# Paired up-projection forms made of unscaled activations during the output projection, with the row factor applied to each pair's results

## The chip, the cores and the metric

The kernel runs on one core of one Trainium2 chip. A core has a matrix engine (PE), whose weight loads (PEld) overlap its matmuls, a vector engine (DVE), a scalar engine (ACT), a general engine (POOL), and a queue engine (SP) that issues transfers. The engines run side by side, each through its own list of instructions in order, and wait for each other by semaphores. Matmul results land in PSUM, in banks of 128 x 512 float32; everything else is in SBUF, with the weights read from HBM. The metric is the device time of one execution in microseconds (us), lower being better.

## The reference

Two layers of a bidirectional encoder over 512 tokens of 1024 features, in float32. What matters here is the second half of a layer and the projection ahead of it:

```python
    x = x + merged @ w_out[l]                      # output projection
    hf = rms_norm(x, ffn_norm_g[l])                # per token: x * rsqrt(mean(x^2) + eps) * g
    u = depthwise_conv(hf @ ffn_w_up[l], ffn_conv_w[l], ffn_conv_b[l])
    u_gate, u_val = u[..., :D_FF], u[..., D_FF:]   # D_FF = 2816
    x = x + (jax.nn.silu(u_gate) * u_val) @ ffn_w_down[l]
```

The convolution runs along the tokens, width 3, one filter per column. Ahead of this stand an input projection, latent attention, grouped-query attention and a pooling branch, merged by gates. The row factor of the norm, rsqrt(mean(x^2) + eps), is one number per token; it can be taken out of the up-projection and put on its result.

## The kernel before

Activations lie feature-major: 8 blocks of 128 features by 512 tokens, `XM`. Each float32 operand of a matmul is held as two halves, a rounded high part and the rest as a low part (`wh`/`wl` or `fh`/`fl` for weights, `HH`/`HL` for the normed input, `ah`/`al` for activations), and each product is three matmuls (`mm3`): high by high, high by low, low by high.

**Output projection.** Eight output blocks of 24 matmuls each. After each block, `norm_steps` runs a chain: residual into `XM` (DVE), high half of XM x g (ACT) and the square (ACT), low half (DVE), sum of squares (POOL). The result is `HH`/`HL`, scaled by the gain g and not yet by the row factor. When all eight squares are summed, `norm_begin` and `norm_finish` make the row factor, `rbc`.

**Up-projection.** Two times 2816 columns are 22 channels (`c`) of 128 gate and 128 value columns each. The channels stand in groups, `SIZES`, and are computed in one of two ways:

- *Plain*, the first group of 6: for gate and value each 8 blocks of 3 matmuls on 512 tokens (`feat_major`), 24 matmuls. `scale` multiplies the result by `rbc` on its way out of PSUM.
- *Paired*, the other 16: a 2 x 2 scheme of fast matrix multiplication over two feature blocks, two halves of the tokens, and gate against value. Seven products (`FORMS`: "11", "12", "1", "22", "2", "4", "3") of 4 x 3 matmuls on 256 tokens take the place of eight. The weights' sums for the forms are made on DVE (`w_form`); the activations' forms (`tf`) are made once a layer by `build_forms`, while the plain channels run: the 8 blocks are normed whole (`hn`), four sums a pair of blocks (`tt`) and the splits follow, with 12 of the 28 forms kept in the `m` tiles, which the attention used before, and 16 in slots.

After either, `convolve` does the convolution (ACT, then two on DVE), the gate (ACT), the product (DVE) and the split of the activation: high half on ACT, low half on POOL.

**Down-projection.** A group's down products are dealt out between the products of the next group's pairs (`_ffn`), and those of the last group come at the end. `keep_act` places a channel's activation: groups 1 to 3 in `HH`/`HL`, group 0 in slots, and the last group's in other tiles.

**Weights.** They come from HBM on SP's queue in an order written out by `_stream`: a raw tile holds two units of 128 x 512, the four raw parts of a pair are tiles of 512 of their own (at most 8 held at once). Each unit is split before use: a "p" unit by a copy on ACT and a subtract on DVE or POOL (`pick`), a "u" unit by two copies on ACT and an accumulating transfer that POOL issues (`by_transfer`). In the plain channels all units are "u". `wnext` splits `LA` = 3 units ahead of use, and `LAF` = 6 where forms are near; six pairs of split tiles rotate.

**Order.** The order on each engine's list is set when the program is written: a model clock (`Clock`) with costs per instruction says when a chain's next step is due, and that is when the instruction is emitted. `PLACE` and `KEEP` place activations and hold back the last downs of a group.

Of the kernel before, what the change touches and what calls it, by code (L numbers as in the profile page):

```python
# [42 lines left out]
LA, LAF = 3, 6  # L43
SIZES = (6, 5, 4, 4, 3)
PLACE = {1: 0, 2: 5, 3: 0}
# [100 lines left out]
def _stream():  # L146


    pieces, slots, units, alone = [], [], [], []
    for kind, *u in _layer_units() * L:  # L150
# [9 lines left out]
        if len(slots) <= KC or alone[-1] or slots[-1] + u[0] > 1024:  # L160
            slots.append(0)
            alone.append(False)
        pieces.append((len(slots) - 1, slots[-1], u[0]))
# [158 lines left out]
def trunk(ctx: ExitStack, tc: tile.TileContext, x, w, prm, gb, cst, out):  # L322
# [101 lines left out]
    def w_split():  # L424
# [22 lines left out]
        if pi + 1 == len(pieces) or pieces[pi + 1][0] > sl:  # L447
# [105 lines left out]
    def norm_steps(gen, kc, g, sq):  # L553
# [17 lines left out]

        return [hi, lo, add]
# [94 lines left out]
    def layer(l, sq, xsrc):  # L667
# [900 lines left out]
        tags = ("acc", "ST", "AV", "mi", "S")  # L1568
        for m in range(KC):
# [13 lines left out]
            chain(resid, *norm_steps(G2, m, col(PRM_FG + m), sq))  # L1583
# [9 lines left out]
        forms = {}  # L1593

        def build_forms():
            for q in range(4):
                m = mp.tile([P, 3, T], F32R, tag="m", name=f"tf{l}{q}")
                forms["raw", q] = m
                for n, name in enumerate(("11", "12", "4")):
                    forms[name, q] = m[:, n, :]  # L1600
                for name in ("1", "22", "2", "3"):
                    forms[name, q] = slot("tf", F32R)[:, :T]
            hn, tt = {}, {}
            lo, hi = slice(0, 256), slice(256, 512)

            def normed(k):
                hn[k] = slot("hn")[:, :T]
                V.scalar_tensor_tensor(hn[k], XM[:, k, :], col(PRM_FG + k), fin["rbc"][:, :T], ALU.mult, ALU.mult)
                done("hn", l, k)

            def sums(q):
# [395 lines left out]
```

## Time and profile before

| What | Value |
|---|---|
| Median of 3 runs | 1577.67 us (1575.77 to 1579.9) |
| The profiled execution's own time | 1578.39 us |
| Its span, first to last instruction | 1576.6 us |
| PE busy | 1548.2 us, 98% |
| DVE / ACT / POOL busy | 1111.4 / 1034.4 / 859.7 us |
| Mean granted PE clock | 0.997 |
| Output projection, layer 0 and 1 | 388 to 432 us, 1170 to 1213 us |
| Plain channels, layer 0 and 1 | 432 to 503 us, 1213 to 1287 us |
| Pairs with dealt downs, layer 0 and 1 | 503 to 765 us, 1287 to 1551 us |

A row of a group of instructions names the line of the kernel, the engine, the operation, what is written and read, shapes and count; then busy us and the mean ns of one; then the engine's idle time just before such instructions and what ended it. A row of the timeline gives start and length in us, and in brackets the idle time before it. Nearly every instruction has the line of a helper (L283 an activation, L290 a two-tensor operation, L294 a three-operand one, L302 a product by scalars, L421 the accumulating transfer, L390 a weight load, L508 a matmul), so the tile's name tells which work it is.

### The profile page before, as it was taken

How to read it: one execution, taken by the hardware profiler on the slowest of the kernel's cores; microseconds unless marked ns; L12 is line 12 of the kernel's file. 1: busy time of each engine (PE TensorE's matmuls, PEld its weight loads, DVE VectorE, ACT ScalarE, POOL GpSimd, SP SyncE). 2: the span in 40 equal slices, each digit the busy share in tenths (PEclk: the TensorE clock that was granted, in tenths of full speed). 3: DMA queues.
4: the chain of work that ended last, by engine and by line, in shares of the span. 5: the costliest groups of instructions: out<-in, count | busy, mean ns of one | idle time of the engine just before them, and what ended most of it. 6: DMA issues, size and time to landing. Idle time of an engine off the chain costs nothing.

```text
span 1576.6 us, 23997 instructions
## 1 busy us (share of the span) xinstructions
PE 1548.2 (98%) x8193; PEld 1338.6 (85%) x8193; DVE 1111.4 (70%) x1816; ACT 1034.4 (66%) x1932; POOL 859.7 (55%) x868
## 2 busy tenths in 40 slices
PE   9999989999999999999999999899999999999999
PEld 8888878888877999998888888788888779999987
DVE  6867886875278777777656688778652877777774
ACT  5557776763478777777655587666535787777773
POOL 3974876854653433333588658668546443333333
PEclk9999999999999999999999999999999999999999
DMA  5432224324489887886535322343244798888853
GB/s 205 126 114 74 74 85 144 107 67 134 113 179 230 200 193 185 205 183 132 135 117 141 100 74 74 96 138 101 70 146 123 170 229 192 192 198 187 194 113 101
DMA packets 127563, 222.36 MB, mean 141 GB/s; under 512 B 29648, under 2 KB 51664, under 8 KB 127440
## 3 DMA queue, kind: packets, MB, share of 16 engines
q1 hardware_dynamic: 90864, 162.93, 33.2%
q0 software_dynamic: 31680, 57.69, 21.3%
q8 instruction: 64, 1.05, 0.3%
q10 hardware_dynamic: 4896, 0.21, 0.2%
q14 instruction: 59, 0.48, 0.1%
HBM read 149.41 MB, written 13.63 MB: 103 GB/s over the span
## 4 chain that ended last, share of the span: by engine, by line
PE 74%; DVE 13%; ACT 6%; issue 4%; POOL 2%; DMA 1%; SPq 0%; ACTq 0%; DVEq 0%; POOLq 0%
PE ps_acc L508 32%; PE ps_AV L508 14%; PE ps_ST L508 12%; PE ps_S L508 8%; PE ps_mi L508 8%; DVE a L294 2%; DVE XM L290 2%; ACT wh L283 1%; DVE wl L290 1%; DVE u L290 1%; DVE mgl L290 1%; ACT mgh L283 1%; DVE hn L294 1%; ACT fh L283 1%; DVE tf L290 1%
## 5 line engine op out<-in xcount | busy, mean ns | idle before, releaser
L290 POOL TENSOR_TENSOR wl<-raw,wh 128x512 fp32r<-128x512 f32 (+3 forms) x241 | 305.0, 1275 | 224.6 <-ACT wh L283 206.5
L283 ACT ACTIVATE wh<-raw 128x512 fp32r<-128x512 f32 (+2 forms) x457 | 269.2, 605 | 56.9 <-DVE raw L290 12.9
L421 POOL DMA_DIRECT2D wl<-raw x124 | 110.9, 919 | 290.3 <-ACT wl L283 106.0
L508 PE MATMUL ps_acc<-HH,wl 128*128 128x512 f32 x416 | 164.3, 395 | 6.2 <-DMA wl<-raw 6.2
L508 PE MATMUL ps_acc<-HH,wh 128*128 128x512 f32 x416 | 164.1, 394 | 3.4 <-DVE vm L290 2.9
L294 DVE SCALAR_TENSOR_TENSOR a<-u,prm,a 128x511 f32<-128x511 f32 x176 | 142.8, 811 | 32.2 <-ACT a L283 31.2
L508 PE MATMUL ps_acc<-HL,wh 128*128 128x512 f32 x416 | 163.5, 393 | 0.0
L421 POOL DMA_DIRECT2D fl<-raw x96 | 85.2, 887 | 105.7 <-ACT sx L283 47.0
L290 DVE TENSOR_TENSOR wl<-raw,wh 128x512 fp32r<-128x512 f32 (+2 forms) x93 | 92.4, 995 | 60.6 <-ACT wh L283 60.5
L283 ACT ACTIVATE a<-u,prm 128x512 f32<-128x512 f32 x88 | 71.5, 815 | 86.6 <-DVE u L290 86.2
L298 DVE TENSOR_REDUCE nm<-ps_S 128x1 fp32r<-128x512 f32 x128 | 87.6, 685 | 36.0 <-PE ps_S L508 34.8
L508 PEld LDWEIGHTS ps_acc<-HH,wl 128*128 128x128 f32 x416 | 78.8, 189 | 24.9 <-DMA wl<-raw 7.9
L508 PEld LDWEIGHTS ps_acc<-HH,wh 128*128 128x128 f32 x416 | 79.0, 190 | 19.8 <-issue 4.4
L508 PE MATMUL ps_AV<-tf,wh 128*128 128x256 f32 x512 | 94.8, 283 | 0.0
L508 PE MATMUL ps_acc<-tf,wh 128*128 128x256 f32 x512 | 94.4, 282 | 0.0
L508 PE MATMUL ps_ST<-tf,fh 128*128 128x256 f32 x512 | 94.2, 281 | 0.0
L508 PEld LDWEIGHTS ps_acc<-HL,wh 128*128 128x128 f32 x416 | 78.9, 190 | 16.3
L508 PEld LDWEIGHTS ps_acc<-tf,wh 128*128 128x128 f32 x512 | 83.9, 191 | 5.3
L508 PEld LDWEIGHTS ps_AV<-tf,wh 128*128 128x128 f32 x512 | 81.4, 190 | 2.6
L283 ACT ACTIVATE wl<-wh 128x512 fp32r<-128x512 f32 x124 | 78.5, 633 | 3.9
L508 PEld LDWEIGHTS ps_ST<-tf,fh 128*128 128x128 f32 x512 | 79.4, 190 | 0.0
L508 PE MATMUL ps_acc<-tf,wl 128*128 128x256 f32 x256 | 72.4, 283 | 0.0
(417 smaller groups left out, 4844.8 us busy)
## 6 DMA issues: line engine op xcount, KB each, us to landing
raw<-w SPq DMA_DIRECT2D x162, 512.0 KB, 3.7
raw<-w SPq DMA_DIRECT2D x136, 256.0 KB, 4.2
wl<-raw POOLq DMA_DIRECT2D x124, 256.0 KB, 4.3
fl<-raw POOLq DMA_DIRECT2D x96, 256.0 KB, 5.4
raw<-w SPq DMA_DIRECT2D x14, 384.0 KB, 3.0
XM<-x SPq DMA_DIRECT2D x16, 256.0 KB, 3.2
dtq<-tr SPq DMA_DIRECT2D x16, 192.0 KB, 1.9
dtk<-tr SPq DMA_DIRECT2D x16, 192.0 KB, 2.0
```

The lines of the kernel that those rows point to most:

```text
L283: return self.eng.activation(out, in_, func, **k)
L290: return self.eng.tensor_tensor(out, *a)
L294: return self.eng.scalar_tensor_tensor(out, *a)
L298: return self.eng.tensor_reduce(out, in_, *a, **k)
L421: nc.gpsimd.dma_start(f(lo), r, accum_op=ALU.add)
L508: PE.matmul(o, lhsT=lhsT, rhs=rhs, start=start, stop=stop, skip_group_check=again)
```

## The change

- One channel a layer goes from plain to paired: groups of 5, 5, 5, 4, 3 instead of 6, 5, 4, 4, 3, so 5 plain channels and 17 pairs.
- The forms are made during the output projection, after each second block, from XM x g without the row factor. `norm_steps` first makes the whole product (`whole`, a product by a column on DVE), then its halves. Forms "11", "12" and "4" are the halves in `HH`/`HL` themselves; the sums and the other 16 forms follow as before.
- Each pair's gate and value results, u and v, are multiplied by `rbc` (`scale`, DVE) before the convolution.
- Activations (down inputs) go into the `m` tiles, six channels' places, and otherwise into wide tiles and slots; `HH`/`HL` stay as they are until the last pair.
- The activations' low halves are made on DVE instead of POOL.
- In the plain channels the second unit of each half channel is a "p" unit; units are split `LAP` = 4 ahead while a "u" is near; and the eight raw tiles of the first two pairs are loaded one after each plain half channel from the second on.

```diff
-SIZES = (6, 5, 4, 4, 3)
-PLACE = {1: 0, 2: 5, 3: 0}
+LA, LAP, LAF = 3, 4, 6
+SIZES = (5, 5, 5, 4, 3)
+PLACE = (0, 5, 0, 5, 0)
+ROOM = 6
...
         if tok[0] == "u":
-            r += [("u", T)] * 2
+            r += [("u", T), ("p", T), ("next",)]
...
+        if kind == "next":
+            plain = (plain + 1) % (2 * SIZES[0])
+            if plain and plain >= 2 * SIZES[0] - 8:
+                early.append(len(slots))
+                slots.append(T)
+                alone.append(True)
+            continue
         if kind == "f":
             if u[1] == FORMS[0]:
-                first = len(pieces)
+                first, fresh = len(pieces), True
                 for _ in range(4):
+                    if early:
+                        pieces.append((early.pop(0), 0, T))
+                        continue
                     pieces.append((len(slots), 0, T))
...
-        n = LAF if any(units[min(i, len(units) - 1)][0] not in "pu" for i in (j, j + LAF)) else LA
+        kinds_ = [units[min(j + i, len(units) - 1)][0] for i in (0, LAP, LAF)]
+        n = LAF if any(k not in "pu" for k in kinds_) else LAP if "u" in kinds_[:2] else LA
...
+        if full is not None:
+            def whole():
+                full[kc] = slot("hn")[:, :T]
+                V.tensor_scalar(full[kc], xk, g, None, ALU.mult)
+
+            def hi_whole():
+                A.activation(hh, full[kc], AF.Copy)
+                A.activation(t[:, :T], xk, AF.Square)
+
+            def lo_whole():
+                V.tensor_tensor(hl, full[kc], f(hh), ALU.subtract)
+                done("H", gen, kc)
+
+            return [whole, hi_whole, lo_whole, add]
...
+        def build_forms(q):
+            a, b = whole.pop(2 * q), whole.pop(2 * q + 1)
...
+            def sums():
+                V.tensor_tensor(t[0][:, lo], a[:, hi], a[:, lo], ALU.subtract)
+                V.tensor_tensor(t[1][:, lo], b[:, hi], a[:, hi], ALU.subtract)
+                V.tensor_tensor(t[0][:, hi], b[:, hi], t[0][:, lo], ALU.subtract)
+                V.tensor_tensor(t[1][:, hi], b[:, lo], t[0][:, hi], ALU.subtract)
+
+            def halves_of(name):
+                i, h = {"1": (0, lo), "2": (0, hi), "3": (1, lo), "22": (1, hi)}[name]
+                d = slot("tf", F32R)[:, :T]
+                forms[name, q] = d[:, lo], d[:, hi]
+
+                def low():
+                    V.tensor_tensor(d[:, hi], t[i][:, h], f(d[:, lo]), ALU.subtract)
+                    done("tf", l, name, q)
+                return [lambda: A.activation(d[:, lo], t[i][:, h], AF.Copy), low]
+
+            for name, k, h in (("11", 2 * q, lo), ("12", 2 * q + 1, lo), ("4", 2 * q + 1, hi)):
+                forms[name, q] = HH[:, k, h], HL[:, k, h]
+                done("tf", l, name, q)
+            chain(sums, *[z for name in ("1", "2", "22", "3") for z in halves_of(name)], after=0.0)
...
-            chain(resid, *norm_steps(G2, m, col(PRM_FG + m), sq))
+            chain(resid, *norm_steps(G2, m, col(PRM_FG + m), sq, whole),
+                  *[lambda m=m: build_forms(m // 2)] * (m % 2))
...
-        chain(([("rbc", G2)], build_forms), after=3.0)
+        places = []
+        for n in range(4):
+            t = mp.tile([P, 3, T], F32R, tag="m", name=f"act{l}{n}")
+            places += [t[:, k, :] for k in range(3)]
...
-            if g in PLACE and PLACE[g] + i < KC:
-                return HH[:, PLACE[g] + i, :], HL[:, PLACE[g] + i, :]
-            if g < len(groups) - 1:
-                return slot("ah", F32R)[:, :T], slot("al", F32R)[:, :T]
+            n = 2 * (PLACE[g] + i)
+            if n < 2 * ROOM:
+                return places[n], places[n + 1]
...
-            return steps + [([("gate", l, c)], prod), *split(ah, al, a[:, :T], eng=G), lambda: done("act", l, c)]
+            return steps + [([("gate", l, c)], prod), *split(ah, al, a[:, :T]), lambda: done("act", l, c)]
...
+            def scale(t):
+                return [([("rbc", G2)], lambda: V.tensor_tensor(t[:, :T], t[:, :T], fin["rbc"][:, :T], ALU.mult))]
...
-                chain(([("s2", l, c)], add(u[:, hi], sa[:, hi], "AV")), *convolve(c, 0, u))
+                chain(([("s2", l, c)], add(u[:, hi], sa[:, hi], "AV")), *scale(u), *convolve(c, 0, u))
             else:
-                chain(([("s4", l, c)], add(v[:, hi], sb[:, lo])), add(v[:, lo], sb[:, hi], "acc"), *convolve(c, 1, v))
+                chain(([("s4", l, c)], add(v[:, hi], sb[:, lo])), add(v[:, lo], sb[:, hi], "acc"), *scale(v), *convolve(c, 1, v))
```

More of the change, by code (lines that the diff above doesn't have):

```diff
@@ L159, in _stream @@
             continue
-        if len(slots) <= KC or alone[-1] or slots[-1] + u[0] > 1024:
+        if len(slots) <= KC or fresh or alone[-1] or slots[-1] + u[0] > 1024:
             slots.append(0)
             alone.append(False)
+        fresh = False
         pieces.append((len(slots) - 1, slots[-1], u[0]))
@@ L446, in w_split @@
         done("w", j)
-        if pi + 1 == len(pieces) or pieces[pi + 1][0] > sl:
+        if pi + 1 == len(pieces) or pieces[pi + 1][0] != sl:
             w_free(sl)
@@ L550, in split, with norm_steps @@
         return steps
-    def norm_steps(gen, kc, g, sq):
+    def norm_steps(gen, kc, g, sq, full=None):
         xk = XM[:, kc, :]
@@ L1710, in product @@
                 need(("tf", l, name, q))
-                ws, d = slice(q * P, q * P + P), forms[name, q]
-                mm3(o, wh[:, ws], wl[:, ws], d[:, 0:256], d[:, 256:512], q == 0 and name in ("11", "12", "1", "22"),
+                ws, (dh, dl) = slice(q * P, q * P + P), forms[name, q]
+                mm3(o, wh[:, ws], wl[:, ws], dh, dl, q == 0 and name in ("11", "12", "1", "22"),
                     q == 3, name not in ("12", "22"))
```

48 lines of the change are left out of this document (4 added, 44 removed).

## The prediction

> **What bounds the kernel now.** I read the page's busy shares first, then who waited for whom on PE in the two feed-forward halves, then the places of those waits in the timeline.
>
> ```profile
> span 1576.6 us, 23997 instructions
> PE 1548.2 (98%) x8193; PEld 1338.6 (85%) x8193; DVE 1111.4 (70%) x1816; ACT 1034.4 (66%) x1932; POOL 859.7 (55%) x868
> ```
>
> PE bounds: at 98% nothing counts that doesn't take matmuls away or close one of PE's holes. The waits of PE, layer 0 (380 to 790 us), then layer 1 (1160 us to the end); columns are total us, times, longest:
>
> ```profile
> PE ps_acc L508 <- DMA wl<-raw: 3.2, 2, 2.5
> PE ps_mi L508 <- POOL HL L290: 2.2, 1, 2.2
> PE ps_ST L508 <- DMA wl<-raw: 0.7, 1, 0.7
> PE ps_mi L508 <- POOL al L290: 0.2, 1, 0.2
> ...
> PE ps_acc L508 <- DMA wl<-raw: 3.0, 1, 3.0
> PE ps_mi L508 <- POOL HL L290: 2.4, 1, 2.4
> PE ps_ST L508 <- DMA wl<-raw: 0.9, 1, 0.9
> ```
>
> Two kinds make nearly all of it: the low half of a plain up weight that a POOL-issued accumulating transfer brings late, and the low half of one activation that POOL subtracts late. PE's timeline at three of them:
>
> ```profile
> 483.88 0.39 PE L508 MATMUL ps_acc<-HL,wh 128*128 128x512 f32 x1
> 486.79 0.50 PE L508 MATMUL ps_acc<-HH,wl 128*128 128x512 f32 x1 [2.52 <-DMA wl<-raw]
> ...
> 725.51 0.40 PE L508 MATMUL ps_mi<-HH,wh 128*128 128x512 f32 x1
> 728.15 0.50 PE L508 MATMUL ps_mi<-HL,wh 128*128 128x512 f32 x1 [2.25 <-POOL HL L290]
> ...
> 1264.76 0.39 PE L508 MATMUL ps_acc<-HL,wh 128*128 128x512 f32 x1
> 1268.11 0.80 PE L508 MATMUL ps_acc<-HH,wl 128*128 128x512 f32 x1 [2.96 <-DMA wl<-raw]
> ```
>
> Stages in the table of windows; columns are length, then busy us (instructions) of PE, PEld, DVE, ACT, POOL, then granted clock, DMA share, GB/s:
>
> ```profile
> 388.20:431.70 43.50, 43.24 (x189) 35.47 (x190) 14.79 (x19) 21.36 (x37) 26.20 (x23) 1.00 0.40 117
> 502.80:569.60 66.80, 66.59 (x452) 61.39 (x451) 48.40 (x78) 50.37 (x93) 24.55 (x27) 1.00 0.88 203
> 487.00:493.00 6.00, 6.00 (x27) 4.94 (x27) 2.12 (x6) 5.87 (x13) 3.34 (x5) 1.00 1.08 230
> 1268.00:1274.00 6.00, 5.89 (x14) 4.64 (x15) 2.03 (x6) 5.88 (x13) 3.50 (x4) 0.51 1.09 228
> ```
>
> They are the output projection, the first four pairs, and the 6 us behind each long weight wait. Behind the wait of 2.52 us PE runs 27 matmuls at clock 1.00, one in 0.222; behind that of 2.96 us only 14 at 0.51. So the first costs 486.79 - 483.88 - 0.22 = 2.7 us, 0.2 over the idle time shown, and the one of layer 1 costs 3.1 and another (27 - 14) x 0.222 = 2.9 behind it.
>
> The Trainium skill ("TensorE: Matmul & The Clock Gate", Part 1) says that a free-running activity window of about 3.4 us halves the clock once one has passed idle. The halving agrees; that 2.52 us kept the clock and 2.96 us lost it agrees with a window whose phase is chance. By that rule the 2.9 us isn't in every execution, and a forecast against the median would gain about half of it, 1.5 us less.
>
> **The change, part by part.**
>
> *One channel per layer goes from plain to paired.* Steps of the chain (start, us, what): a plain half channel of 24 matmuls, and a product of 12.
>
> ```profile
> 399.97 5.44 PE ps_AV L508 x24
> 522.52 1.43 PE ps_AV L508 x12
> ```
>
> Plain: 2 x 5.44 = 10.88. Paired: 7 x 1.43, at most 1.44, = 10.05. Gain 0.83 a layer, **1.7 us** in all. The paired form's seven weight sums lie on DVE, ACT and POOL.
>
> *Plain weights.* Every second half of a plain weight goes from an accumulating transfer (two ACT copies, a POOL issue, a transfer) to an ACT copy and a subtract; the splits start 4 units ahead rather than 3; and the eight 256 KB loads for the first two pairs are spread over the plain channels instead of standing at their end. POOL in the plain stage (432.2 to 502.8), the transfers' landing there (431.7 to 497.5), POOL's issue for the 483.88 wait, ACT's copies in the same stretch, and POOL's weight subtracts in the output projection (388.2 to 431.7):
>
> ```profile
> L421 POOL DMA_DIRECT2D wl<-raw x21 | 19.4, 993 | 27.7 <-ACT tf L283 16.3 <-ACT wl L283 10.4 <-ACT fh L283 0.7
> L290 POOL TENSOR_TENSOR al<-a,ah 128x512 fp32r<-128x512 f32 x5 | 10.1, 2024 | 2.5 <-ACT ah L283 2.5
> ...
> wl<-raw POOLq DMA_DIRECT2D x21, 256.0 KB, 5.0
> raw<-w SPq DMA_DIRECT2D x9, 256.0 KB, 6.5
> ...
> 480.01 0.89 POOL L421 DMA_DIRECT2D wl<-raw  x1 [2.74 <-ACT tf L283]
> ...
> L283 ACT ACTIVATE wh<-raw 128x512 fp32r<-128x512 f32 x21 | 12.9, 617 | 3.3 <-DMA raw<-w 3.3
> ...
> L290 POOL TENSOR_TENSOR wl<-raw,wh 128x512 fp32r<-128x512 f32 x14 | 18.0, 1290 | 14.4 <-ACT wh L283 11.6 <-PE ps_acc L508 1.8 <-PE ps_ST L508 1.0
> ```
>
> The late one is issued at 480.01 and used at 486.79, 6.8 us, beside the burst of 256 KB loads. A unit is 12 matmuls of 0.227, 2.72 us: the lead is 8.2 us now and 10.9 after. Two ACT copies (1.3 us with the hand-over), up to 1 us until the issue, and 6.8 us are about 9: over 8.2, under 10.9. A subtract on POOL needs 0.62 + 1.29, some 2 us with its copy. POOL also loses the 5 activation subtracts it does there, ACT and DVE most of the form-making, so issues come earlier. I take both layers' weight waits as gone: layer 0, 2.7 + 2 x 0.9 (the rest of its 3.9 us of waiting, 0.2 added to each) = **4.5**; layer 1, 3.1 + 2.9 + 1.1 = **7.1**. What stays if I am wrong: POOL's in-order queue now holds 10 subtracts of 1.3 us ahead of 10 issues, and pieces of 1 us may remain, so I keep 0 to 5 us a layer and charge 0.7 each.
>
> *Activation low halves from POOL to DVE, and the row factor as two more DVE products a pair.* DVE rows: plain stage (432.2 to 502.8), then pairs (502.8 to 700.7), with POOL's row of the pairs last:
>
> ```profile
> L294 DVE SCALAR_TENSOR_TENSOR hn<-XM,prm,rbc 128x512 f32<-128x512 f32 x8 | 6.0, 745 | 0.0
> L290 DVE TENSOR_TENSOR tf<-tt,tf 128x256 fp32r<-128x256 f32 x16 | 6.2, 419 | 3.9 <-ACT tf L283 3.9
> ...
> L290 DVE TENSOR_TENSOR wl<-raw,wh 128x512 fp32r<-128x512 f32 x24 | 23.3, 970 | 17.0 <-ACT wh L283 17.0
> L290 DVE TENSOR_TENSOR a<-a,a 128x512 f32<-128x512 f32 x12 | 8.2, 684 | 0.0
> ...
> L290 POOL TENSOR_TENSOR HL<-a,HH 128x512 fp32r<-128x512 f32 x10 | 15.2, 1521 | 3.2 <-ACT HH L283 3.2
> ```
>
> Added per pair: 3 x 0.684 = 2.05 us. The window 502.8 to 569.6 holds four pairs with their downs, 16.7 us and 12.1 of DVE each: 72% becomes at most 85%. Part returns: a 128x512 product takes 0.684, but the weight subtract beside POOL's work 0.970; if that excess is the collision with POOL's subtracts, 24 x 0.29 over 12 pairs is 0.6 us a pair back. PE has no wait on DVE there now, and I charge none.
>
> The wait at 725.51 is for channel 18's low half. Its chain on DVE, ACT and POOL:
>
> ```profile
> 717.52 0.42 DVE L290 TENSOR_TENSOR u<-ps_acc,sx 128x256 f32<-128x256 f32 x1
> 719.05 0.74 DVE L294 SCALAR_TENSOR_TENSOR a<-u,prm,a 128x511 f32<-128x511 f32 x1
> 721.91 0.68 DVE L290 TENSOR_TENSOR a<-a,a 128x512 f32<-128x512 f32 x1
> ...
> 723.74 0.62 ACT L283 ACTIVATE HH<-a 128x512 fp32r<-128x512 f32 x1
> ...
> 726.52 1.58 POOL L290 TENSOR_TENSOR HL<-a,HH 128x512 fp32r<-128x512 f32 x1
> ```
>
> With the row factor everything behind 717.94 moves by about 0.7: the ACT copy ends at 725.1, DVE's subtract at 725.8 against a need at 725.74. Behind ACT, POOL now loses 2.2 us that DVE need not; but DVE's queue may hold something ahead, up to the 2.2. I charge 0.7 a layer. Gain: 2.5 + 2.6 (and perhaps 0.8 of slow clock behind the second, an estimate from the row above: a quarter of its 2.9) + 0.5 (the small al wait) - 1.4 = **5.0**. What is late next is the last group's channel at the layer's end, where the same exchange (0.68 more, 0.9 less) leaves it as it is; 0.4 a layer for luck.
>
> *Forms built in the output projection.* The nearest row for a product by a column (from the first 300 us), and POOL's sums of squares (388.2 to 431.7):
>
> ```profile
> L302 DVE TENSOR_SCALAR gb<-gb 128x128 f32<-128x128 f32 x2 | 0.3, 210 | 0.0
> ...
> L290 POOL TENSOR_TENSOR sq<-sq,sqt 128x512 f32<-128x512 f32 x6 | 8.3, 1388 | 0.0
> ```
>
> Added there on DVE for each pair of blocks: two whole products by a column (not in the trace in this form; between 0.210, which is a quarter of the width, and 0.745, a full-width product of two tensors; I take 0.5), four sums and four low halves of 0.419; on ACT four copies.
>
> That is 4.4 us a pair of blocks, 17 in all, on 14.79 busy of 43.5: it fits. On the path is the last block alone: residual, whole product, copy, low half before the first plain channel's last matmuls, 21 x 0.227 = 4.8 us later. Four steps of 0.5 to 0.75 with hand-overs are about 3.3 us, so nothing, or up to 2 us if DVE is held; I charge 0.5 a layer. Squares, the mean's factor and SP's queue keep their order; the eight early loads are the same bytes. Activations in the attention's tiles wait for nothing that isn't long over, and the normalized halves now stay until the last pair, before the next layer's are written.
>
> **Sum** against this execution (span 1576.6, its time 1578.39, 0.7 above the median 1577.67): 1.7 + 4.5 + 7.1 + 5.0 = 18.3 gained, less 2 x (0.7 + 0.4 + 0.5) = 3.2: 15.1 us. 1578.4 - 15.1 = 1563.3; the 0.7 down to the median are about made up by the slow-clock stretch, which other executions need not have had: **1563 us**.
>
> **Rivals.**
>
> *The weights are still late (1570).* Ten transfers remain in each plain stage. Against: the lead above. For: eight loads now run beside every one of them, DMA share 0.88 in the next stage. If half of the 11.6 stays and a microsecond of slow clock comes with it: 1563 + 5.8 + 1 = 1570.
>
> *DVE and POOL hold each other up in the output projection (1570).* POOL's subtracts in the plain stage take 2.02 us, in the output projection 1.29: something holds them when DVE is busy. If no DVE instruction of two inputs may run beside a POOL one, then from 399 to 432 POOL's 12 weight subtracts and 6 sums, 18 x 1.29 = 23.2, and DVE's 24 x 0.419 + 6 x 0.75 + 6 x 0.5 = 17.6 make 41 us in 33. The lead of 8.2 us swallows most of 8 us; 3 or 4 us a layer come through: 1563 + 7 = 1570. The Trainium skill ("SBUF — State Buffer") states just such an exclusive lock on the port pair that the two engines share, held for a whole instruction. By that the part is slower, but the pairs, rid of POOL's subtracts, gain.
>
> *DVE becomes the bound in the pairs (1585, slower).* Place: 17 pairs a layer, 34 in all; price: what PE waits per pair. It decides from 15.1 / 34 = 0.44 us a pair; at 0.7 it is 1563 + 24 = 1587, about 1585. It needs DVE near 16.7 us a pair, or its queue held by a result that comes later than the order written out assumes. Against: 14.1 of 16.7, and no wait now.
>
> *The gain is given back by a new order (1576).* The planner's clock shifts every later choice, the second attention's too; several waits of a microsecond would eat most.
>
> **How the numbers follow.** Forecast 0.50; late weights 0.19; the port 0.11; given back 0.09; DVE bound 0.11. Anything within 0.3% (4.7 us) can't be told from no change. Faster takes the first three, 0.80; same 0.09; slower 0.11. Low end: all charges nil and 2 us of luck in the later order, 1563 - 3 - 4 = 1556; high end, to leave out no more than the slow case and part of the given-back one, 1577. The likeliest case alone spans 1557 to 1567.
>
> **What would show it.** Right: no wait of PE on wl by DMA over 0.5 us in the plain stages; plain stage of about 54.5 us against 70.6; no POOL row writing an activation's low half; pairs at 16 to 17 us without a PE wait on DVE; layer 1's clock at 1.00 throughout. Wrong: waits of PE on DVE tiles in the pairs, on wl in the output projection, or on HL at the first plain channel, and remaining waits on transfers that were issued under 7 us ahead.

## The result and the profile after

| | Before | After |
|---|---|---|
| Median of 5 runs each | 1577.67 us (1575.31 to 1579.9) | 1571.23 us (1569.27 to 1574.29) |
| The profiled execution's own time | 1578.39 us | 1569.55 us |
| Its span | 1576.6 us | 1567.7 us |

The ratio is 0.9959, with a 95% interval of 0.9941 to 0.9978: faster by 0.4%. The gain is 6.4 us between the medians and 8.8 us between the two profiled executions, where 15.1 us had been forecast. The sign and the range were right, the size less than half.

The head and the line of engines of the page of after:

```profile
span 1567.7 us, 24155 instructions
PE 1546.2 (99%) x8265; PEld 1339.0 (85%) x8265; DVE 1171.7 (75%) x1932; ACT 1012.9 (65%) x1908; POOL 809.8 (52%) x822
```

PE is busy 2.0 us less than before and still the bound; the other 6.9 us of the span come from its idle time. What PE waits for in the two feed-forward halves (total us, times, longest), layer 0 and then layer 1:

```profile
PE ps_acc L522 <- DMA wl<-raw: 1.3, 2, 1.0
PE ps_acc L522 <- ACT HH L296: 0.6, 1, 0.6
...
PE ps_acc L522 <- DVE HL L303: 0.2, 1, 0.2
...
PE ps_acc L522 <- DMA wl<-raw: 3.0, 2, 2.3
...
PE ps_acc L522 <- DVE HL L303: 0.2, 1, 0.2
```

The waits for POOL's low halves are gone altogether, 2.2 + 0.2 and 2.4 us as listed before. The waits for transferred weights have shrunk and moved, and two waits are new: for the halves of the normed input itself, `HH` and `HL`. PE's timeline shows where the ones of layer 0 stand:

```profile
434.98 0.50 PE L522 MATMUL ps_acc<-HH,wl 128*128 128x512 f32 x1 [1.00 <-DMA wl<-raw]
...
440.17 0.51 PE L522 MATMUL ps_acc<-HH,wh 128*128 128x512 f32 x1 [0.58 <-ACT HH L296]
...
440.90 0.51 PE L522 MATMUL ps_acc<-HL,wh 128*128 128x512 f32 x1 [0.22 <-DVE HL L303]
```

All three lie in the first 8 us of the plain stage, which begins at 433.4: the very first transferred weight, and then the last of the eight blocks. Layer 1 has 2.3 us at the first weight and the same 0.2 for `HL`, none for `HH`; one weight wait more in each layer, 0.3 and 0.7 us, comes later in the stage. The stages in the table of windows (length; busy us and instructions of PE, PEld, DVE, ACT, POOL; granted clock, DMA share, GB/s), namely the output projection, the plain stage and the pairs of layer 0, and the plain stage of layer 1:

```profile
389.20:433.40 44.20, 43.97 (x193) 36.06 (x194) 33.14 (x43) 20.89 (x41) 27.02 (x22) 1.00 0.37 117
433.40:491.40 58.00, 55.86 (x243) 44.96 (x242) 41.19 (x63) 36.77 (x63) 28.91 (x25) 1.00 0.77 192
491.40:762.00 270.60, 270.60 (x1860) 251.64 (x1858) 216.68 (x366) 201.98 (x376) 76.85 (x88) 1.00 0.78 174
...
1211.20:1270.50 59.30, 56.05 (x244) 44.89 (x243) 42.12 (x63) 36.76 (x63) 28.80 (x25) 1.00 0.75 187
```

In the pairs PE is busy for all of 270.60 us: nothing holds it there, DVE at 80% included. Five plain channels are 10 x 5.44 = 54.4 us of matmuls, so the plain stages (58.05 and 59.27 by PE's first and last matmul) lose 3.65 and 4.87 us, together 8.5. Before, by the same reckoning with 65.3 us for six channels, 70.37 and 73.10 lost 5.1 and 7.8, together 12.9. So this term brought 4.4 us. The granted clock is 1.00 in every stage; the slow stretch of before (0.95 over its layer 1 stage) has gone from this execution. It is not gone from every one: of the five executions of after, the two longest, 1571.44 and 1574.29 us, have mean clocks of 0.997 and 0.996 and the two shortest 1.000.

The output projection shows what is new there. DVE's sums in its groups between 399 and 440 us (busy us, mean ns), then DVE, POOL and ACT in the timeline (start, length, in brackets the idle time before), in order of time:

```profile
L303 DVE TENSOR_TENSOR tt<-hn,hn 128x256 f32<-128x256 f32 x3 | 3.4, 1142 | 0.0
L303 DVE TENSOR_TENSOR tt<-hn 128x256 f32<-128x256 f32 x3 | 3.3, 1095 | 0.0
```

```profile
422.36 0.48 DVE L315 TENSOR_SCALAR hn<-XM,prm 128x512 f32<-128x512 f32 x1
...
422.87 0.63 ACT L296 ACTIVATE HH<-hn 128x512 fp32r<-128x512 f32 x1 [3.30 <-DVE hn L315]
...
426.24 0.63 ACT L296 ACTIVATE wl<-wh 128x512 fp32r<-128x512 f32 x1
...
427.32 1.48 POOL L303 TENSOR_TENSOR wl<-raw,wh 128x512 fp32r<-128x512 f32 x1
427.57 1.51 DVE L315 TENSOR_SCALAR hn<-XM,prm 128x512 f32<-128x512 f32 x1
428.75 1.05 POOL L434 DMA_DIRECT2D wl<-raw  x1
...
431.69 1.46 POOL L303 TENSOR_TENSOR wl<-raw,wh 128x512 fp32r<-128x512 f32 x1
431.92 1.51 DVE L303 TENSOR_TENSOR tt<-hn,hn 128x256 f32<-128x256 f32 x1
...
437.94 0.68 DVE L307 SCALAR_TENSOR_TENSOR XM<-ps_ST,XM 128x512 f32<-128x512 f32 x1
```

The sums of 128x256 take 1.10 to 1.14 us in the mean, where an operation of that form took 0.419 in the plain stage of before; the one at 431.92 takes 1.51. A product by a column takes 0.48 us at 422.36 and 1.51 at 427.57. Both ran into a weight subtract of POOL that had begun 0.23 to 0.25 us earlier, and both end 0.28 us after it: 428.80 and 429.08, 433.15 and 433.43. The second instruction does its work when the first is done. POOL pays too: 1.48 where it took 1.29. The Trainium skill ("SBUF — State Buffer", Who interferes with whom) says that DVE and GpSimd share a pair of ports under an exclusive lock, that whoever issues first keeps it for its whole instruction, and that a `tensor_scalar` can take part by its two-port mode; the trace agrees in each point that these rows can show.

Two things follow, both to be read in these rows. PE finishes the last block at about 433.4, and its residual starts on DVE at 437.94, 4.5 us later, because DVE is still at the sums and halves of the blocks before; so `HH` and `HL` are late. And the late product at 422.36 holds up ACT: it stands idle for 3.30 us before the copy of that block, and the copies of the first transferred weight stand behind it in ACT's order. They end at 426.87, a subtract of POOL stands ahead of the issue, and the first transfer of the plain stage is issued at 428.75, 4.6 us before that stage begins; it lands 6.2 us later.

### The profile page after: what moved, and what is told of

It is laid out like the page before. It is cut to its first block, busy times and chain, and to the rows that moved or that the text cites. A ratio compares the mean times of both kernels' runs of the same rounds, so it can differ in the third digit from the quotient of the medians.

```text
span 1567.7 us, 24155 instructions
## 1 busy us (share of the span) xinstructions
PE 1546.2 (99%) x8265; PEld 1339.0 (85%) x8265; DVE 1171.7 (75%) x1932; ACT 1012.9 (65%) x1908; POOL 809.8 (52%) x822
## 3 DMA queue, kind: packets, MB, share of 16 engines
q8 instruction: 65, 1.06, 0.3%
## 4 chain that ended last, share of the span: by engine, by line
PE 84%; DVE 7%; issue 3%; ACT 3%; POOL 2%; DMA 1%; SPq 0%; ACTq 0%; POOLq 0%; DVEq 0%
PE ps_acc L522 35%; PE ps_AV L522 16%; PE ps_ST L522 14%; PE ps_S L522 10%; PE ps_mi L522 10%; DVE XM L303 1%; DVE tt L303 1%; POOL wl L303 1%; DMA wl<-raw 1%; DVE mgl L303 1%; ACT mgh L296 1%; DVE sq L303 0%; DVE gt L307 0%; ACT wh L296 0%; DVE XM L307 0%
## 5 line engine op out<-in xcount | busy, mean ns | idle before, releaser
L303 POOL TENSOR_TENSOR wl<-raw,wh 128x512 fp32r<-128x512 f32 (+3 forms) x261 | 335.6, 1292 | 273.3 <-ACT wh L296 252.7
L434 POOL DMA_DIRECT2D wl<-raw x96 | 83.7, 872 | 246.8 <-ACT sx L296 160.4
L307 DVE SCALAR_TENSOR_TENSOR a<-u,prm,a 128x511 f32<-128x511 f32 x176 | 133.7, 761 | 34.9 <-ACT a L296 34.1
L522 PE MATMUL ps_acc<-tf,wh 128*128 128x256 f32 x544 | 100.1, 282 | 0.0
L303 DVE TENSOR_TENSOR wl<-raw,wh 128x512 fp32r<-128x512 f32 (+2 forms) x97 | 71.7, 740 | 25.5 <-ACT wh L296 25.3
L522 PE MATMUL ps_AV<-HH,wh 128*128 128x256 f32 (+1 forms) x248 | 82.1, 331 | 0.0
L522 PE MATMUL ps_AV<-HH,wl 128*128 128x256 f32 (+1 forms) x248 | 82.0, 331 | 0.0
L522 PE MATMUL ps_AV<-HL,wh 128*128 128x256 f32 (+1 forms) x248 | 82.0, 331 | 0.0
L296 ACT ACTIVATE ps_ST<-ps_ST 128x512 f32<-128x512 f32 x86 | 49.8, 581 | 33.1 <-PE ps_ST L522 31.7
L296 ACT ACTIVATE fl<-fh 128x512 fp32r<-128x512 f32 x102 | 64.5, 633 | 3.2
```

What stands on the lines that cost most here:

```text
L296: return self.eng.activation(out, in_, func, **k)
L303: return self.eng.tensor_tensor(out, *a)
L307: return self.eng.scalar_tensor_tensor(out, *a)
L434: nc.gpsimd.dma_start(f(lo), r, accum_op=ALU.add)
L522: PE.matmul(o, lhsT=lhsT, rhs=rhs, start=start, stop=stop, skip_group_check=again)
```

## The experiments

My theory after this comparison: the gain is that of the forecast, and the meeting of DVE and POOL in the output projection takes some 6 us of it. The rivals: DVE's queue is too full there, whoever else is busy; or the early loads delay the transfers; or the weights' new split and lead fall short. The ratio is against the kernel before in the same series; the last two columns are the plain stages in us by PE's matmuls.

| Kernel | Median us | Ratio [95%] | Layer 0 | Layer 1 |
|---|---|---|---|---|
| before | 1577.67 | 1 | 70.37 | 73.10 |
| after | 1571.23 | 0.9959 [0.9941, 0.9978] | 58.05 | 59.27 |
| e1_forms_later | 1565.08 | 0.9920 [0.9904, 0.9936] | 55.57 | 54.65 |
| e2_out_sub_dve | 1563.49 | 0.9918 [0.9897, 0.9939] | 55.81 | 55.27 |
| c1_sub_dve_from_m1 | 1564.37 | 0.9901 [0.9887, 0.9916] | 55.77 | 55.23 |
| e8_before_dve_act (6 plain) | 1566.56 | 0.9923 [0.9901, 0.9945] | 66.67 | 70.95 |
| e6_pool_act | 1589.62 | 1.0062 [1.0047, 1.0077] | 61.19 | 62.15 |
| e9_pool_act_on_e2 | 1583.65 | 1.0028 [1.0017, 1.0040] | 58.90 | 58.56 |
| e4_all_subtract | 1580.25 | 1.0009 [0.9999, 1.0020] | 62.03 | 62.25 |
| e5_uu_on_e2 | 1564.93 | 0.9905 [0.9890, 0.9919] | 55.49 | 54.65 |
| e7_lap3_on_e2 | 1566.30 | 0.9914 [0.9898, 0.9931] | 54.88 | 54.92 |
| c2_sub_dve_lap3 | 1565.09 | 0.9917 [0.9902, 0.9932] | 54.73 | 54.67 |
| e3_loads_late | 1570.87 | 0.9959 [0.9944, 0.9974] | 59.89 | 58.59 |
| e10_before_dve_act_spread (6 plain) | 1564.13 | 0.9895 [0.9876, 0.9914] | 66.91 | 66.57 |

### What took half of the gain

**e1_forms_later**: the changed kernel, with the forms built behind the output projection.

```diff
-            chain(resid, *norm_steps(G2, m, col(PRM_FG + m), sq, whole),
-                  *[lambda m=m: build_forms(m // 2)] * (m % 2))
+            chain(resid, *norm_steps(G2, m, col(PRM_FG + m), sq, whole))
...
+        for q in range(4):
+            at(8.0 + 6.0 * q, lambda q=q: build_forms(q))
```

> The changed kernel, but the four sums and the splits of the forms start 8 us into the plain channels instead of during the output projection; whole products stay where they are. Port theory (a DVE instruction with two SBUF inputs and a POOL subtract hold each other up): in the output projection POOL's weight subtracts come back from 1.34 us to 1.29, the first accumulating transfer of the plain weights is issued about 2 us sooner (428.8 to about 427), and the waits of PE for HH and HL of the last block (0.74 + 0.5 us in layer 0, 0.5 in layer 1) are gone; plain stages of 58.0 and 59.3 us fall to about 56 and 57, the time by about 4 us. If only the transfers' landing counts: HH and HL waits go, the waits for wl stay, 1.5 us less. Rival (the forms are harmless and the whole product alone delays HH and HL): no change of the waits.

It took 1565.08 us, 6 less than the changed kernel. Its plain stage of layer 1 in the windows, and POOL's first issue for the plain stage of layer 0, which begins at 432.82:

```profile
1208.90:1263.60 54.70, 54.70 (x244) 45.30 (x243) 45.88 (x76) 36.04 (x66) 25.55 (x21) 1.00 0.72 182
```

```profile
423.44 1.03 POOL L434 DMA_DIRECT2D wl<-raw  x1
```

The waits for `HH`, `HL` and the first weight are gone, layer 1's stage has no stall at all, and POOL's subtracts are back at 1.30 us. The first transfer is issued 9.4 us ahead of its stage instead of 4.6, in both layers; so the first weight's wait had the same source as those of the halves. The first pairs take 0.7 and 2.7 us longer, as the forms now come late for them. This run moves the forms and with them DVE's work; it doesn't yet tell the meeting of two engines from a queue that is full.

**e2_out_sub_dve**: the changed kernel, with all weight subtracts of the output projection on DVE. DVE does more, POOL less.

```diff
-            e = V if j < KC + 3 else pick(W_BIAS, ck.fin + ck.SEM)
+            e = V if j < KC + 3 or st.get("out") else pick(W_BIAS, ck.fin + ck.SEM)
...
+        st["out"] = True
...
-        st["ffn"] = True
+        st["ffn"], st["out"] = True, False
```

> The changed kernel, but in the output projection all weight subtracts are done on DVE instead of on POOL. Port theory: the form sums there fall from 0.86 us each to about 0.42 and the form splits from 0.73 to about 0.42, since POOL has only the squares' sums left; HH and HL of the last block come in time although DVE does 11 us more of work; the first transfer is issued 2 to 3 us sooner; the time falls by 3 to 5 us. Rival (DVE's queue is simply too full, no collision): HH and HL come later still, the waits at the first plain channels grow from 1.2 to 3 us or more a layer, the time rises.

It took 1563.49 us. The window of its output projection of layer 0, two of DVE's groups between 399 and 440, and POOL's first issue for the plain stage, which begins at 432.88:

```profile
388.10:432.90 44.80, 44.22 (x193) 36.05 (x194) 37.48 (x61) 22.24 (x44) 9.01 (x8) 1.00 0.45 136
```

```profile
L303 DVE TENSOR_TENSOR tt<-hn,tt 128x256 f32<-128x256 f32 x6 | 2.5, 420 | 0.1
...
L303 DVE TENSOR_TENSOR tt<-hn,hn 128x256 f32<-128x256 f32 x3 | 1.2, 415 | 0.0
```

```profile
422.85 1.06 POOL L434 DMA_DIRECT2D wl<-raw  x1 [6.82 <-ACT tf L296]
```

DVE is busier in the output projection than in after (37.48 against 33.14 us, with 18 instructions more; POOL has 8 instead of 22), and yet most of its sums are back at 0.415 to 0.420 (the forms' low halves, at 0.674 in the mean, and the products by a column, at 0.864, are not), the last block's halves come in time, and the first transfer is issued 10.0 us ahead of its stage. That speaks against the queue that is merely too full: the engine with more to do is done sooner. What stays in the plain stages is one wait for a transferred weight of 0.6 us in layer 0 and 0.3 in layer 1.

**c1_sub_dve_from_m1**: e2, but the first output block keeps POOL's subtracts, because e2 opens the output projection with a wait of 0.35 us for another tile.

```diff
+            st["out"] = m > 0
```

> A candidate: as the run with the weight subtracts of the output projection on DVE, but only from its second block on, since that run's output projection had become 44.8 us long instead of 44.2, with a wait for the last merged block at its start. Port theory: output projection back to 44.2, plain stages as in that run (55.8 and 55.3 us), so 0.5 to 1.2 us faster than it: 1562 to 1563 us. If the first block's subtracts on POOL delay the rest, nothing is gained.

The output projections are back at 44.17 and 44.22 us (44.79 and 44.78 in e2), the plain stages stay as in e2. The times of c1 and e2 can't be told apart; either is about the forecast's 1563.

### Which part made the gain

**e8_before_dve_act**: the kernel before with one word changed, the activations' low halves on DVE.

```diff
-            return steps + [([("gate", l, c)], prod), *split(ah, al, a[:, :T], eng=G), lambda: done("act", l, c)]
+            return steps + [([("gate", l, c)], prod), *split(ah, al, a[:, :T]), lambda: done("act", l, c)]
```

> The kernel before with a single part of the change: the activations' low halves on DVE. If POOL's queue, held by those subtracts, was what made the plain weights' transfers late: the waits of PE for wl in the plain stages (4.5 us in layer 0, 7.1 with the slow clock in layer 1) shrink to under 2 us a layer, and the waits for POOL at the last boundary (2.5 and 2.6 us) go; time down by 8 to 14 us. If the short lead, the burst of loads or the forms on ACT and DVE in the plain stage were the cause: the boundary waits go, the waits for wl stay; time down by 4 to 6 us.

0.9923: 12 us, more than the whole change. The window of its pairs in layer 0:

```profile
498.90:760.00 261.10, 260.18 (x1777) 241.01 (x1776) 185.68 (x317) 195.01 (x358) 75.09 (x86) 1.00 0.80 181
```

It has the same six plain channels, the same two copies and transfer for each weight, the same lead of 3 units: yet the plain stages are 3.7 and 2.2 us shorter, although one wait for a weight of 2.8 us stays in layer 1, and the pairs at the groups' boundaries, 18.07 and 19.75 us before, take 15.55. DVE, with 17 instructions more in that stretch of pairs, is busy 185.68 us there; before it was 192.39 in a stretch of nearly the same length:

```profile
502.80:765.00 262.20, 259.74 (x1776) 240.72 (x1775) 192.39 (x300) 195.70 (x358) 96.16 (x103) 1.00 0.80 179
```

How does a subtract of an activation make a weight late? The issue that the prediction showed at 480.01 comes 47.6 us into its stage before and 43.6 in e8, while the first fourteen issues for the stage agree to 0.02 us. Around the first that differ, the timeline of before, POOL, DVE and ACT, has this:

```profile
463.76 3.72 POOL L290 TENSOR_TENSOR al<-a,ah 128x512 fp32r<-128x512 f32 x1
...
467.43 0.86 POOL L421 DMA_DIRECT2D wl<-raw  x1
467.69 2.49 DVE L294 SCALAR_TENSOR_TENSOR a<-u,prm,a 128x511 f32<-128x511 f32 x1
468.05 1.56 POOL L290 TENSOR_TENSOR al<-a,ah 128x512 fp32r<-128x512 f32 x1
...
472.88 0.81 ACT L283 ACTIVATE a<-u,prm 128x512 f32<-128x512 f32 x1 [3.48 <-DVE u L290]
...
476.42 0.86 POOL L421 DMA_DIRECT2D wl<-raw  x1 [5.06 <-ACT tf L283]
```

A first subtract of POOL takes 3.72 us, and the issue behind it, at 467.43, comes 1.3 us later in its stage than in e8: that much is POOL's own queue. Its transfer lands at 473.03, and PE waits 0.7 us for it; two issues on, the delay is made up. Then DVE's step of 467.69 runs beside an issue and the second subtract and takes 2.49 us where it is 0.74 a few rows on; ACT waits 3.48 us for DVE, with the weights' copies behind it, and the issue of 476.42 is 2.2 us late after POOL has stood idle for 5.06. At the issue of 480.01, 4.0 us late, POOL had been idle for 2.74 us, waiting for ACT. So the transfer that made PE wait longest was not late because POOL's queue was full: DVE was held, then ACT, and POOL waited.

**e6_pool_act** and **e9_pool_act_on_e2**: the reverse edit, POOL given the activations' low halves again, once in the changed kernel and once in e2.

```diff
-            return steps + [([("gate", l, c)], prod), *split(ah, al, a[:, :T]), lambda: done("act", l, c)]
+            return steps + [([("gate", l, c)], prod), *split(ah, al, a[:, :T], eng=G), lambda: done("act", l, c)]
```

> The changed kernel with one part undone: the activations' low halves on POOL again. The forecast put 5.0 us on this part, for the waits of PE at the boundary of the last two groups. If so, a wait of 2 to 3.5 us for POOL comes back in each layer (longer than before the change by the 0.7 us of the row factor), DVE's subtracts of weights in the pairs go from 0.7 back to about 1.0 us, and the time rises by 4 to 8 us. Rival (the new group sizes alone moved the boundary out of the way): no such wait, time within 2 us.

> The run with the output projection's subtracts on DVE, with the activations' low halves put back on POOL. If those subtracts hold POOL's queue: waits for wl of 0.4 to 1.1 us each in the plain stages as in the changed kernel with that part undone, plain stages at 57 to 59 us against 55.8 and 55.3, waits for POOL at the boundaries of 4 us a layer, time up by 12 to 18 us. If the plain waits of that run came from the crowded output projection: plain stages stay within 1 us of 55.5, and only the boundary waits come, 8 to 10 us in all.

e6 took 1589.62 us and e9 1583.65, that is 18 and 20 us over the kernels they were made from (16 and 17 by the ratios), where 4 to 8 had been expected of e6 and 12 to 18 of e9. PE's waits in layer 0 of e9:

```profile
PE ps_mi L522 <- POOL act L303: 3.9, 2, 2.2
PE ps_acc L522 <- DMA wl<-raw: 2.3, 2, 1.1
PE ps_AV L522 <- DMA wl<-raw: 0.9, 1, 0.9
```

The boundary wait is back as it was to be, and with it the waits for transferred weights, under the new lead and the new kinds of units alike. The place where e9 leaves e2 in the plain stage, first e9 and then e2, 1.7 us apart by their stages' starts:

```profile
463.21 3.16 DVE L307 SCALAR_TENSOR_TENSOR a<-u,prm,a 128x511 f32<-128x511 f32 x2 [2.51 <-ACT a L296]
463.44 1.58 POOL L303 TENSOR_TENSOR act<-a,act 128x512 fp32r<-128x512 f32 x1
...
467.12 0.63 ACT L296 ACTIVATE act<-a 128x512 fp32r<-128x512 f32 x1 [3.95 <-DVE a L303]
```

```profile
461.52 1.54 DVE L307 SCALAR_TENSOR_TENSOR a<-u,prm,a 128x511 f32<-128x511 f32 x2 [1.72 <-ACT a L296]
...
463.81 0.63 ACT L296 ACTIVATE act<-a 128x512 fp32r<-128x512 f32 x1 [2.33 <-DVE a L303]
```

Two DVE steps take 3.16 us instead of 1.54, ACT waits 1.6 longer, and from there the issues come 1.6 and then 3.3 to 3.8 us later. POOL's subtract lies within DVE's two steps: it is the meeting of DVE and POOL again, passed on by ACT. So one part of the change made the whole term of the boundaries and a good part of that of the plain weights: of the 12.9 us that the plain stages of before lose, e8 takes away 5.9, and in e9 6.4 come back. The 7.0 us that e8 still loses have another source, in part the loads (see e10).

### The split, the lead and the loads

**e4_all_subtract**: the changed kernel, both units of a plain half channel copied and subtracted, none transferred.

```diff
-            r += [("u", T), ("p", T), ("next",)]
+            r += [("p", T), ("p", T), ("next",)]
```

> The changed kernel, but all plain weights are split by a copy and a subtract, none by an accumulating transfer (lead back to 3 units, as for all such units). If the remaining waits for wl (1.3 + 0.6 us in layer 0, 2.6 + 1.0 in layer 1) are the transfers' own: they are all gone, plain stages of 55.5 to 56.5 us, 5 us less in all. Port theory: POOL's 20 subtracts of 1.3 us collide with DVE's work in the plain stage, DVE's convolution steps grow from 0.76 us; as long as this stays under the stage's 54 us the time still falls; if not, waits of PE for DVE or POOL tiles of 1 us and more take the place.

That missed: the weight waits do go, but the time is 1580.25. PE's wait at the last block, and the plain stage of layer 0:

```profile
442.27 0.80 PE L522 MATMUL ps_acc<-HH,wh 128*128 128x512 f32 x1 [4.68 <-ACT HH L296]
```

```profile
432.60:494.70 62.10, 57.42 (x244) 46.62 (x243) 48.89 (x61) 31.90 (x56) 35.05 (x26) 0.95 0.44 136
```

More subtracts on POOL and DVE at the end of the output projection hold up the forms there even more, 4.68 us at `HH` (DVE's product of the last block, at 440.07, takes 1.48 us behind a subtract of POOL begun at 439.83), and the long wait costs some clock behind it (0.95). It is the theory's mechanism again, at several times the size, where I had looked for its absence.

**e5_uu_on_e2**: e2 with both units by transfer, as before the change. **e7_lap3_on_e2** and **c2_sub_dve_lap3**: e2 and c1 with the lead of 3 as before the change.

```diff
-            r += [("u", T), ("p", T), ("next",)]
+            r += [("u", T), ("u", T), ("next",)]
...
-LA, LAP, LAF = 3, 4, 6
+LA, LAP, LAF = 3, 3, 6
```

> The run with the subtracts of the output projection on DVE, with the change's split of the plain weights undone: all units by accumulating transfer, lead still 4. If the split by kind is what took the waits for wl away: waits of 1 to 3 us a layer come back in the plain stage, time up by 3 to 6 us. If the longer lead did it: waits stay under 1 us a layer, time within 2 us.

> The run with the subtracts of the output projection on DVE, with the lead of the plain units put back from 4 to 3. If the lead took the waits for wl away: the transfers that land in 6 to 7 us come after their 8.2 us of lead less the copies, each slow one costs 0.5 to 2 us, plain stages grow by 2 to 5 us each, time up by 4 to 10 us. If the split by kind alone did it: plain stages within 1 us.

> A candidate: subtracts of the output projection on DVE from its second block on, and the lead of the plain units back at 3. From the stages of the two runs: output projection 44.2, plain stages 54.9, so 1 us a layer under the run with the lead of 4; 1561 to 1564 us, if the wait of 1.5 us for a residual at each layer's end, which came with the lead of 3, doesn't show up again.

The plain stage of layer 1 in e5 (c2 has 54.73 and 54.67 us in the table):

```profile
1210.90:1265.60 54.70, 54.70 (x244) 45.33 (x243) 35.59 (x60) 39.99 (x68) 22.62 (x23) 1.00 0.99 236
```

That stage of e5 and both stages of c2 have no stall left at all: twice the transfers at a DMA share of 0.99, or the old lead, and PE is busy from end to end. Neither the kind of unit nor the lead is worth anything that can be measured once the queue is free; the intervals of e2, e5, e7, c1 and c2 overlap. With the lead of 3, a wait of 1.5 us of PE for the residual `XM` stands at each layer's end in e7 and c2; why the order moves so stays open.

**e3_loads_late**: the changed kernel, the eight early loads again at the end of the plain stage.

```diff
-            if plain and plain >= 2 * SIZES[0] - 8:
+            if False:
```

> The changed kernel, but the eight 256 KB loads of the first two pairs stand at the end of the plain channels again, as before the change. If a load that starts together with an accumulating transfer is what makes that transfer slow (6 to 7 us against 3.5): the transfers' landing in the first three quarters of the plain stage comes down to 3.5 to 5 us, the first wait for wl (1.0 and 2.3 us) shrinks by 1 to 2 us, and a new wait of 1 to 3 us stands at the end of the plain stage, where the eight loads come together. If it is the late issue alone: landing times and the first wait stay as they are, and only the end gets worse.

1570.87, the same as after. PE's waits in layer 0:

```profile
PE ps_ST L522 <- DMA wl<-raw: 1.4, 1, 1.4
PE ps_acc L522 <- ACT HH L296: 1.2, 1, 1.2
```

The first weight comes sooner (a wait of 0.33 for 1.0), the wait for `HH` is longer (1.2 for 0.6), and a wait of 1.4 comes late in the stage. By the stages layer 0 loses 1.8 us and layer 1 gains 0.7; in the time no difference shows.

**e10_before_dve_act_spread**: e8 with the eight loads spread as in the change, all else as before.

```diff
-            r += [("u", T)] * 2
+            r += [("u", T), ("u", T), ("next",)]
...
+                    if early:
+                        pieces.append((early.pop(0), 0, T))
+                        continue
```

> The kernel before with two parts of the change: the activations' low halves on DVE, and the eight 256 KB loads of the first two pairs spread over the plain channels. With the first part alone the waits left in the plain stages are 0.8 us at 466 in layer 0 and 2.8 us plus a stretch at half clock at 1267 in layer 1, the latter for a transfer that took 8.0 us beside the burst of loads. If the burst is its cause: plain stages of 66.7 and 71.0 us become about 66 each, the time falls by 3 to 5 us, to 1562 to 1564, which would be the fastest kernel here. If spreading only moves the collision: transfers of 6 us and more through the whole plain stage, waits of about 1 us in other places, the time within 2 us of 1566.6.

1564.13 us, ratio 0.9895. PE's waits for weights, layer 0 and layer 1:

```profile
PE ps_ST L520 <- DMA wl<-raw: 1.1, 1, 1.1
...
PE ps_ST L520 <- DMA wl<-raw: 0.4, 1, 0.4
```

The 2.8 us of e8 in layer 1, for a transfer that landed in 8.0 us beside the burst of loads, is down to 0.4, and that stage from 70.95 to 66.57; layer 0 stays as it was (66.67, 66.91). So the spread is worth something where a burst meets a transfer that is needed soon: the plain stages lose 2.9 us in all where e8 loses 7.0. The stages show that, and not the times alone, whose intervals overlap. This kernel, without the change's forms, channels or places, beats both kernels of the case; so do e2 and c1.

## Why the prediction was right or wrong

**The failed step** is in "Forms built in the output projection": "it fits", with "nothing, or up to 2 us if DVE is held; I charge 0.5 a layer". I added up DVE's time alone, 17 us on 14.79 of 43.5. What counts is the sum of the instructions of both engines that can't run side by side. The forecast had that sum in its rival, 41 us in 33, priced at 1570 and given a chance of 0.11; the time came to 1571. Against c1 the plain stages of after are 2.3 and 4.0 us longer: 6.3 us for a charge of 1.0. The rival's "3 or 4 us a layer come through" was about right in size. I had the row that spoke for it, POOL's 2.02 against 1.29, and by it the rival should have been the forecast.

**Plain weights**, forecast 11.6 less 1.4: 4.4 us in after, and 10.7 in c1, where the plain stages lose only 55.77 + 55.23 - 2 x 54.4 = 2.2 of the former 12.9. The size was right for a kernel without that meeting. The reason was wrong: I gave it to the split by kinds, the lead of four and the spread loads, and named POOL's lost subtracts last, as work out of the way of the issues. e5, e7 and c2 show the first two, each undone alone, worth nothing measurable. The spread took 4.1 us from the plain stages of e8, and nothing that shows from the time of after (e3). The last was worth 5.9 to 6.4 us (e8, e9), though in the main by way of DVE and ACT and not of POOL's queue.

**Activation low halves**, forecast 5.0 less 0.8: right in its mechanism, and low in size. The pairs at the boundaries cost 18.07 - 15.55 = 2.5 and 19.75 - 15.55 = 4.2 us, the small wait for `al` 0.5; all are gone, 7.2 us in all. Of the 4.2, about 1.6 are slow clock behind the wait, where I had put 0.8. That the weight subtract's 0.970 us in the pairs was a collision with POOL was right too; DVE's row in the pairs of after:

```profile
L303 DVE TENSOR_TENSOR wl<-raw,wh 128x512 fp32r<-128x512 f32 x26 | 17.8, 686 | 4.3 <-ACT wh L296 4.2
```

0.970 has become 0.686. So the same mechanism was read rightly in one stage and dismissed in another.

**One channel from plain to paired**, forecast 1.7: about -1.6. The 0.83 us a layer are there, but each pair takes 0.05 to 0.12 us longer: with 10 downs dealt into it 17.03 us against 16.91, with 8 of them 15.60 to 15.66 against 15.55, over 16 pairs 1.2 and 1.4 us in the two layers. The last pair with the downs behind it takes 37.9 us against 37.5 and 37.6. So two layers' 1.7 become -1.6. PE waits for nothing in there. The chain's pieces have a slower beat; a piece of nine matmuls of downs of before, and one of after (start, us, matmuls):

```profile
550.75 2.07 PE ps_mi L508 x9
```

```profile
656.28 2.10 PE ps_mi L522 x9
```

A down matmul takes 2.07 / 9 = 0.230 us before and 2.10 / 9 = 0.233 after. The beat is the same in every kernel made from the changed one, in e6 too, where POOL does the activations, and in e1, where the forms are made later; it is the old one in e8 and e10. So it goes with what the kernels of the change share, the places of forms and activations among it, and not with POOL's load or the time of the forms. The cause stays open.

**The sum**: 4.4 + 7.2 - 1.6 is 10.0 us. The profiled executions differ by 8.8; 1.0 of the difference is that this output projection starts at 389.20 rather than 388.20, ahead of anything the change touches.

**The other rivals.** DVE as the bound in the pairs: wrong, no wait there. Late weights: part of what remains, but as an effect of the output projection. Given back by the order: 1.5 us at a layer's end in e7 and c2, nothing of the sort in after. The slow stretch of layer 1 was gone from the profiled execution, as the forecast had it. The low end of the range takes off 4 us of luck where its words have 2; by the words it is 1558, and nothing hangs on it.

**The signs named**: POOL writes no activation's low half, pairs of 15.6 to 17.0 us, no PE wait on DVE in them, clock 1.00 all came. Of the others, a plain stage of 54.5 us and no wait on `wl` over 0.5 failed to come (58 us, and waits of 1.0 and 2.3), and the wait on `HL` at the first plain channel was listed as a sign of a wrong forecast; together they named the place.

## What to carry to other kernels

Where two engines hold each other up, price a move by the sum of both engines' work in that stage, and not by the free time of the one that receives it; the sign to look for is one instruction with two durations in two stages. When a transfer is late, follow its issue back through the queues of the engines that prepare it, to the first instruction that takes longer than its like, before giving it more lead: one kind of subtract moved from POOL to DVE was worth 12 to 20 us here, more lead nothing. And where a change has many parts, the part that pays may be one word, and the rest may take back half.

## What the runs showed of the hardware that was not expected

A one-input product by a column takes part in the meeting of DVE and POOL: 0.48 us alone, 1.51 behind a subtract. In e2, without POOL's subtracts, it met an issue (the one at 422.85, 1.06 us long, shown above) and a sum of POOL in a row. DVE and then POOL in the timeline of e2:

```profile
422.92 2.62 DVE L315 TENSOR_SCALAR hn<-XM,prm 128x512 f32<-128x512 f32 x1
```

```profile
423.64 1.61 POOL L303 TENSOR_TENSOR sq<-sq,sqt 128x512 f32<-128x512 f32 x1
```

It took 2.62 us and ended at 425.54, 0.29 after POOL's sum. It had started ahead of that sum and still ended behind it, so the issue of a transfer seems to count as well. DVE's step at 467.69 in the kernel before is alike: begun beside an issue, ahead of a subtract, and ended 0.57 behind it. No run tests the issue by itself.

A 256 KB accumulating transfer landed in 3.7 us where no load was issued within 2 us of it (e8, 475.85), and in 6.2 with loads of 512 and 256 KB issued 0.1 and 0.5 us behind it (after, 428.75); the one that layer 1 of e8 waits for took 8.0 beside the burst of loads.

And waits of 2.8 us (e8, layer 1) and 4.68 us (e4) each lowered the stage's mean clock, to 0.98 and 0.95, while the 2.3 us of after left it at 1.00. The length alone does not decide: in the kernel before, PE's wait of 2.37 us at 1511.82 is followed by a mean of 0.72 from 1512 to 1518, and that of 2.52 by 1.00.
